# Expert layer's start: second stream's seed matmuls spread over the waits, two turned tiles in another bank, expert 0's overflow test behind expert 1's start

## Chip, core and metric

One core of a Trainium2 chip runs the kernel. The metric is the device time of one execution in microseconds; the figures shown are the median and the spread of several executions. Engine names are those of the profile: PE (TensorE matmul) and PEld (its weight load), DVE (VectorE), ACT (ScalarE), POOL (GpSimd), SP (SyncE, which here issues nearly all DMAs).

## What is computed

One layer of a hybrid model on 256 tokens of 1024 channels, float32. Four mixers and an output projection come first; then, as far as the change goes:

```python
x = x + g1 * y_x
h_x = modulate(rmsnorm(x, norm2_g), sh2, sc2)
logits = (h @ w_router + b_router)            # 256 tokens, 32 experts
top_vals, top_idx = lax.top_k(logits, 4); gates = softmax(top_vals)
# per expert e, on the tokens that chose it:
gu = xb @ w_gu[e] + b_gu[e]                   # 1024 x 2048
act = (min(up, 7) clipped + 1) * swish-like(gate)
y = act @ w_down[e] + b_down[e]               # 1024 x 1024
x = x + g2 * sum of gates * y ; return rmsnorm(x, final_norm_g)
```

All 32 experts run, so all their weights (12 MB each, 384 MB) are read once.

## The kernel before

**Weights.** The expert weights are a stream of 384 chunks of 1 MB, 12 for an expert: 8 of `w_gu` (one for each of the 8 rows of 128 of the contraction) and 4 of `w_down`. The text calls them chunk 0 to 383; chunk 12e + k belongs to expert e. They go through a ring of 18 places in SBUF (`RING`, `NSLOT`), so chunk n + 18 goes where chunk n was and can be issued only when the last reader of chunk n in the program before it is done. `load_to(n)` appends the chunks up to n to SP's queue. SP works strictly in the order of its queue: a DMA that waits for its place holds all DMAs behind it. Eight DMAs can be under way (eight semaphores in turn). Places 16 and 17 of the list, the last in the ring's order, hold the two tensors `YT` (input of the output projection, chunk 16's place) and `XT` (the residual stream, transposed, chunk 17's place) until they have been read for the last time.

**Up to the first expert** (lines 795 to 1050). `finish(b)` ends the output projection and puts the new stream into `XT`, two tiles of 128 channels at a time. `natural(i)` turns tile i back to tokens on partitions, into PSUM banks 4 to 7. `squares` sums squares on ACT, `logits` multiplies by the router; a square root on ACT and a short Newton step on DVE give the norm `rs2`. DVE then makes the logits `LG`, the eight largest (`max`), a mask of the top four (`match_replace`, `MK`, its copy `MB` in bf16), PE ranks the tokens of each expert by matmuls with triangular ones (lines 871 to 875), and DVE makes of the rank `PM` a one-hot matrix (line 911). `pick` (line 929) gathers the tokens of an expert by matmul with the one-hot from `H`, the normed stream, which ACT copies out of the banks of `natural`. `picked` copies the result to SBUF, `turn_rows` transposes it and DVE applies scale and shift: `XET`, the input of `gate_up`. `seed(c)` multiplies the stream's tiles by the identity into the four banks in which the experts' outputs are summed up later; it is the last reader of `XT`.

**The experts.** `gate_up(e)` (line 956) is 32 matmuls (64 in the profile, since float32 takes two passes), `down(e)` (line 980) half as many. An expert has room for 64 tokens. If more chose it, `block(e, 64)` runs the expert a second time on the rest; that is a branch on a count, taken at run time by PE, DVE and ACT (`tc.If`, line 1060). In each turn e of the loop stands, in this order: `down(e - 1)`, the loads of the next chunks, the test and block of expert e, the sum of expert e - 1, `gate_up(e)`, the pick of the next expert, the swish, the next turn of rows and of the activations. So before the first `gate_up` PE meets the test of expert 0.

A chunk's readers, in the order of the program, are the block of its expert (when it is taken) and `gate_up` or `down` of it. Where the branch is not taken, PE adds what the block would have added to its semaphore, once all of its work ahead of the branch is done.

Of the kernel before, what the change touches and what calls it, by code (L numbers as in the profile page):

```python
# [10 lines left out]
ALU = mybir.AluOpType  # L11
# [56 lines left out]
def tile_hybrid_moe(tc, x, ctx, vec, mats, const, pos_col, pos_row, rows, bias, w_mod, w_in, w_out,  # L68
# [4 lines left out]
    with tc.tile_pool(name="big", bufs=1) as big, tc.tile_pool(name="acc", bufs=1, space=PSUM) as acc_pool, \  # L73
# [10 lines left out]
        def R(off, n):  # L84
            return B[:, off:off + n]
# [719 lines left out]
        def natural(i):  # L805

            for c in range(2):
                pe.transpose(N[c][i // 4][:, (i % 4) * P:(i % 4 + 1) * P], XT[:, i, c * P:(c + 1) * P], ident)

        def seed(c):  # L810

            for i in range(KT):
                pe.matmul(Y[c][i // 4][:, (i % 4) * P:(i % 4 + 1) * P], XT[:, i, c * P:(c + 1) * P], ident,
                          start=(i % 4 == 0), stop=False)

        def logits(k):
# [26 lines left out]
        dve.scalar_tensor_tensor(ssq[:, 0, :], ssq[:, 0, :], EPS, ssq[:, 1, :], op0=ALU.add, op1=ALU.add)  # L843
# [4 lines left out]
        w2 = ssq[:, 0, :]  # L848
        dve.tensor_tensor(out=w2, in0=w2, in1=ssq[:, 2, :], op=ALU.add)
        rsqrt_newton(rs2, w2, tn2)  # L850
        act.activation(SM[:, 1:2], epsc, AF.Exp)
        for c in range(2):
            dve.scalar_tensor_tensor(LG[:, c, :], LR[:, c, :], rs2[:, c:c + 1], LB, op0=ALU.mult, op1=ALU.add)
            for q in range(2):
                act.activation(H[:, c, cols2[q]], N[c][q], AF.Copy, scale=rs2[:, c:c + 1])
            dve.max(out=M8[:, c, :], in_=LG[:, c, :])
        dve.tensor_scalar(nm, M8[:, :, 0], -1.0, None, op0=ALU.mult)
# [74 lines left out]
        def picked():  # L932
            act.activation(XE, mis[0], AF.Copy)  # L933

        def turn_rows(dst, ps):
# [3 lines left out]
            d4 = dst.rearrange("p j (g s) -> p j g s", g=2)  # L939
            dve.tensor_tensor(out=d4, in0=ps.rearrange("p (j g s) -> p j g s", j=4, g=2),  # L940
                              in1=jg(A2c).unsqueeze(3).to_broadcast([P, 4, 2, CAP]), op=ALU.mult)
            dve.tensor_tensor(out=d4, in0=d4, in1=jg(SH2c).unsqueeze(3).to_broadcast([P, 4, 2, CAP]), op=ALU.add)
# [307 lines left out]
```

## Time and profile before

| | |
|---|---|
| median of 3 executions | 1122.84 us (1119.83 to 1123.47) |
| profiled execution | 1123.31 us, of which span 1121.4 us |
| PE busy | 1036.5 us, 92% of the span |
| DVE, ACT, POOL busy | 305.3, 128.7, 34.9 us |
| DMA | 445.47 MB, mean 397 GB/s |

Times in the profile count from the start of the span. The parts of the span: up to some 160 us the mixers and the output projection, then some 12 us up to the first `gate_up`, then 32 experts. In one expert the branch is taken, at about 386 us. A table by windows gives for each stretch the busy time of the engines, the clock that TensorE was granted (1.00 is 2.4 GHz, 0.50 is 1.2 GHz) and the rate at which the DMA engines moved bytes.

### The profile page before, as it was taken

The page shows a single profiled execution, that of the slowest core. Times are in us where ns is not written, and L with a number is a line of the kernel's source. Part 1 is how long each engine was busy: PE and PEld are TensorE (multiplying, and loading weights), DVE is VectorE, ACT ScalarE, POOL GpSimd, SP SyncE. Part 2 cuts the span into 40 slices and gives each one's busy share as a digit, 9 for nine tenths or more (in the row PEclk, how much of TensorE's full clock was granted, in tenths as well). Part 3 has the DMA queues.
Part 4 walks back from the last instruction along what each step waited for, and adds up shares of the span by engine and source line. Part 5 has one row for each costly group of instructions (what it writes and reads, how often), then busy time and mean ns, then how long its engine had stood idle before and what let it go on. Part 6 is the DMA issues. An engine that isn't in the chain of part 4 may idle for free. (4 is left out here: it accounts for less than half of the span.)

```text
span 1121.4 us, 12287 instructions
## 1 busy us (share of the span) xinstructions
PE 1036.5 (92%) x4888; PEld 424.1 (38%) x4888; DVE 305.3 (27%) x588; ACT 128.7 (11%) x239; POOL 34.9 (3%) x77
## 2 busy tenths in 40 slices
PE   4999989999999989999999998999989898989995
PEld 2665864333333333333333333333323232323232
DVE  5488742122222212221212121212121112111122
ACT  4133430000000000000000000000000000000002
POOL 4102120000000000000000000000000000000000
PEclk8999998999999999999999999999999999999999
DMA  9987988999999998999999999999999999999994
GB/s 293 375 352 314 411 335 337 391 419 420 420 420 421 422 389 356 420 421 420 419 420 421 420 421 420 420 420 420 421 420 420 422 420 419 421 420 420 421 405 159
DMA packets 71148, 445.47 MB, mean 397 GB/s; under 512 B 7748, under 2 KB 9732, under 8 KB 20360
## 3 DMA queue, kind: packets, MB, share of 16 engines
q1 hardware_dynamic: 70408, 443.44, 96.5%
q8 instruction: 71, 1.16, 0.4%
q0 software_dynamic: 640, 0.63, 0.2%
q14 instruction: 29, 0.24, 0.1%
HBM read 442.40 MB, written 1.05 MB: 395 GB/s over the span
## 5 line engine op out<-in xcount | busy, mean ns | idle before, releaser
L956 PE MATMUL bank<-B 128*64 128x512 f32 x2112 | 473.4, 596 | 35.4 <-DMA B<-in_w_gu_dram 34.1
L956 PEld LDWEIGHTS bank<-B 128*64 128x64 f32 x2112 | 160.4, 137 | 329.1 <-issue 224.2
L980 PE MATMUL bank<-B 128*64 128x512 f32 x1024 | 228.2, 598 | 2.7 <-DMA B<-in_w_down_dram 1.8
L960 DVE TENSOR_SCALAR B<-bank 128x512 f32<-128x512 f32 x33 | 22.8, 692 | 464.3 <-issue 404.0
L980 PEld LDWEIGHTS bank<-B 128*64 128x64 f32 x1024 | 71.6, 138 | 139.7 <-issue 127.6
L961 ACT ACTIVATE B<-B 128x512 f32<-128x512 f32 x33 | 20.8, 630 | 765.6 <-DVE B L960 765.6
L1004 DVE TENSOR_TENSOR B<-bank,B 64x512 f32<-64x512 f32 x64 | 44.0, 688 | 223.1 <-PE bank L980 222.3
L1008 PE MATMUL bank<-B 128*128 128x512 f32 (+2 forms) x140 | 69.7, 606 | 3.2 <-PEq L1107 2.3
L929 PE MATMUL bank<-B 128*64 128x512 f32 x264 | 63.4, 599 | 0.9 <-DVE B L866 0.9
L945 PE MATMUL bank<-T,E 96*64 96x512 bf16 x196 | 33.6, 389 | 6.4 <-PEq L1060 4.8
L1008 PEld LDWEIGHTS bank<-B 128*128 128x128 f32 x140 | 22.7, 191 | 38.3 <-issue 25.7
L380 PE MATMUL bank<-B 128*128 128x256 f32 x160 | 36.8, 385 | 0.0
L940 DVE TENSOR_TENSOR B<-bank,B 128x512 f32<-128x512 f32 x33 | 22.8, 692 | 42.7 <-PE bank L937 42.7
L929 PEld LDWEIGHTS bank<-B 128*64 128x64 f32 x264 | 20.4, 137 | 36.6 <-issue 35.6
L380 PEld LDWEIGHTS bank<-B 128*128 128x128 f32 x160 | 30.9, 194 | 8.4 <-issue 4.5
L945 PEld LDWEIGHTS <-E 96*64 96x64 bf16 x196 | 10.6, 106 | 46.1 <-issue 45.1
L973 ACT ACTIVATE B<-bank 128x512 f32<-128x512 f32 x33 | 19.7, 597 | 55.8 <-PE bank L972 55.8
L933 ACT ACTIVATE B<-bank 128x512 f32<-128x512 f32 x33 | 19.7, 597 | 47.5 <-PE bank L929 47.5
L937 PEld LDWEIGHTS bank<-B 128*128 128x128 f32 x132 | 16.5, 143 | 22.4 <-ACT B L933 20.6
L962 DVE TENSOR_SCALAR B<-bank 128x512 f32<-128x512 f32 x33 | 22.8, 692 | 3.7 <-PE bank L956 0.6
L964 DVE SCALAR_TENSOR_TENSOR B<-B 128x512 f32<-128x512 f32 x33 | 22.8, 692 | 3.4
L535 DVE SCALAR_TENSOR_TENSOR B<-B 128x256 f32<-128x256 f32 x58 | 23.2, 481 | 0.0
(273 smaller groups left out, 534.3 us busy)
## 6 DMA issues: line engine op xcount, KB each, us to landing
B<-in_w_gu_dram SPq DMA_DIRECT2D x256, 1024.0 KB, 19.8
B<-in_w_down_dram SPq DMA_DIRECT2D x127, 1024.0 KB, 20.0
B<-in_w_mod_dram SPq DMA_DIRECT2D x16, 1024.0 KB, 6.6
B<-in_w_mod_dram SPq DMA_DIRECT2D x16, 512.0 KB, 10.0
B<-in_w_out_dram SPq DMA_DIRECT2D x4, 1024.0 KB, 8.9
B<-in_w_in_dram SPq DMA_DIRECT2D x8, 384.0 KB, 7.6
B<-in_w_in_dram SPq DMA_DIRECT2D x8, 256.0 KB, 5.4
B<-in_ctx_dram SPq DMA_DIRECT2D x1, 1024.0 KB, 6.2
```

Of the source, the lines that this page charges most:

```text
L380: pe.matmul(half(b, t), w, UT[:, k, 256:512], start=(k == 0 and t == 0), stop=(k == KT - 1 and t == 1))
L535: dve.scalar_tensor_tensor(dst, src, w, dst, op0=ALU.mult, op1=ALU.add)
L929: pe.matmul(mis[0][64 * g:64 * g + 64, :], p[:, c, :], H[:, c, 512 * g:512 * g + 512], start=(c == 0), stop=(c == 1))
L940: dve.tensor_tensor(out=d4, in0=ps.rearrange("p (j g s) -> p j g s", j=4, g=2), in1=jg(A2c).unsqueeze(3).to_broadcast([P, 4, 2, CAP]), op= ...
L945: pe.matmul(dst[64 * g:64 * g + 64, :], E3[:, e:e + 1].to_broadcast([96, CAP]), T[:, col:col + 512], start=True, stop=False)
L956: pe.matmul(dst[64 * g:64 * g + 64, :], xt[:, k % 4, (k // 4) * 64:(k // 4) * 64 + 64], w[:, b * 1024 + g * 512:b * 1024 + g * 512 + 512], ...
L960: dve.tensor_scalar(GH, G0, 7.0, 0.5, op0=ALU.min, op1=ALU.mult)
L962: dve.tensor_scalar(UP, G1, 7.0, -7.0, op0=ALU.min, op1=ALU.max)
L964: dve.scalar_tensor_tensor(UP, TH, 1.0, UP, op0=ALU.add, op1=ALU.mult)
L980: pe.matmul(dst[64 * g:64 * g + 64, :], AT[:, k % 4, (k // 4) * 64:(k // 4) * 64 + 64], dn[e, k, g], start=False, stop=(k == KT - 1))
L1004: dve.tensor_tensor(out=dst[p0:p0 + 64, 512 * g:512 * g + 512], in0=ps[64 * g:64 * g + 64, :], in1=G2B[64 * g:64 * g + 64, :], op=ALU.mult)
L1008: pe.matmul(Y[c][q][:, a:b], s[:, c * P:(c + 1) * P], o[:, 512 * q + a:512 * q + b], start=False, stop=last)
```

## The change

- `natural(6)` and `natural(7)` write to bank 2 (`N6`, free since `finish(2)`) in place of the second halves of banks 5 and 7. Their squares stand ahead of the copy of the logits on ACT.
- The mask: the top four are copied to a tile `W8` whose other entries are set at the start; `MB` comes straight from the comparison in bf16; the memset and the cast between them are gone. The load of the exponential's table on ACT stands behind the copies of `H`, of which there are now six.
- The one-hot of the first pair of experts is made in two instructions of half the size; the pick of expert 0 waits for the first.
- `turn_rows` of expert 0 works in two halves, and `gate_up(0)` takes the chunks in the order 0, 1, 4, 5, 2, 3, 6, 7.
- The seed matmuls, before eight tiles of one token half at a time, are spread: tiles 4 to 7 behind the router's second product, 0 and 1 ahead of the pick, 2 and 3 behind it, tiles 0 to 2 of the second half behind the turned rows, tiles 3 to 7 behind `gate_up(0)` and the pick of expert 1.
- Chunk 17, whose place is `XT`, is loaded by a `load_to` behind these last seeds; before the loop stands `load_to(NSLOT - 1)`.
- Expert 0's test and block stand in turn 1, behind `down(0)` and ahead of the loads of that turn.

The diff, cut to its core:

```diff
-        def seed(c):
-            for i in range(KT):
+        def seed(c, tiles_):
+            for i in tiles_:
                 pe.matmul(Y[c][i // 4][:, (i % 4) * P:(i % 4 + 1) * P], XT[:, i, c * P:(c + 1) * P], ident, ...)
...
         for k in range(4, KT):
             logits(k)
+        squares(2, N6)
         act.activation(LT, bank[0][:, 0:256], AF.Copy)
...
-        squares(2, 1, 256, 512)
-        seed(0)
+        seed(0, range(4, KT))
         rsqrt_newton(rs2, w2, tn2)
-        act.activation(SM[:, 1:2], epsc, AF.Exp)
         for c in range(2):
             dve.scalar_tensor_tensor(LG[:, c, :], LR[:, c, :], rs2[:, c:c + 1], LB, op0=ALU.mult, op1=ALU.add)
...
-        dve.memset(M8[:, :, TOPK:8], 3.0e38)
         for c in range(2):
-            dve.match_replace(out=MK[:, c, :], in_to_replace=M8[:, c, :], ...)
-        dve.tensor_tensor(out=MK, in0=MK, in1=LG, op=ALU.not_equal)
-        dve.tensor_copy(MB, MK)
+            dve.tensor_copy(W8[:, c, 0:TOPK], M8[:, c, 0:TOPK])
+            dve.match_replace(out=MK[:, c, :], in_to_replace=W8[:, c, :], ...)
+        dve.tensor_tensor(out=MB, in0=MK, in1=LG, op=ALU.not_equal)
+        dve.tensor_tensor(out=MK, in0=MK, in1=LG, op=ALU.not_equal)
+        act.activation(SM[:, 1:2], epsc, AF.Exp)
...
-        one_hot(0)
+        for i in range(2):
+            dve.tensor_tensor(out=PP[0][:, :, i, :], ...)
+        seed(0, range(2))
+        pick(PP[0][:, :, 0, :])
+        picked()
+        seed(0, range(2, 4))
         gates(0)
         gates(1)
...
-        pick(PP[0][:, :, 0, :])
-        picked()
-        turn_rows(XET, mis[1])
-        seed(1)
+        turn_rows(XET, mis[1], 2)
+        seed(1, range(3))
...
-        load_to(NSLOT)
+        load_to(NSLOT - 1)
...
-            if e < NE - 2:
-                r = nc.values_load(CNT[0:1, e:e + 1], ...)
+            tests = [(i, nc.values_load(CNT[0:1, i:i + 1], ...))
+                     for i in ([0, 1] if e == 1 else [e] if 0 < e < NE - 2 else [])]
             if e > 0:
                 down(e - 1, mis[1])
+            for i, r in tests[:-1]:
+                with tc.If(r > CAP):
+                    block(i, CAP)
+            if e > 0:
                 load_to(e * NCH + NSLOT)
-            if e < NE - 2:
+            for i, r in tests[-1:]:
                 with tc.If(r > CAP):
-                    block(e, CAP)
+                    block(i, CAP)
...
             picked()
+            if e == 0:
+                seed(1, range(3, KT))
+                load_to(NSLOT)
```

Three places show how the instructions now stand. The first is SP's queue at chunks 12 to 24 (L568 loads `w_gu`, L582 `w_down`; the branch row marks where the test of expert 0 stands in the queue, and SP does not wait at it). Before:

```order
L568 DMA B<-in_w_gu_dram 128x2048 x3
L1060 UNCONDITIONAL_BRANCH
L568 DMA B<-in_w_gu_dram 128x2048 x5
L582 DMA B<-in_w_down_dram 128x2048 x4
L568 DMA B<-in_w_gu_dram 128x2048
```

After the change:

```order
L568 DMA B<-in_w_gu_dram 128x2048 x6
L1074 UNCONDITIONAL_BRANCH
L568 DMA B<-in_w_gu_dram 128x2048 x2
L582 DMA B<-in_w_down_dram 128x2048 x4
L568 DMA B<-in_w_gu_dram 128x2048
```

The order of the chunks is the same, but the branch of expert 0, which stood between chunks 14 and 15, now stands between chunks 17 and 18: in the program, chunk 18 comes behind expert 0's block.

The second place is PE from the ranks (the bf16 row) to the first expert. L929 is the pick, L937 the turned rows, L813 the seeds (banks 2 and 3 first token half, 6 and 7 second), L1055 and L1060 the test. Before:

```order
L875 MATMUL bank_71<-MB,OB 32x32
L929 MATMUL bank_70<-B 64x512 x4
L937 MATMUL bank_71<-B 128x128 x4
L813 MATMUL bank_76<-B 128x128 x4
L813 MATMUL bank_77<-B 128x128 x4
L1055 TENSOR_LOAD CNT
L1055 ISA x2
L1060 COMPARE_AND_BRANCH
```

After the change (L935 pick, L943 turned rows, L818 seeds, L953 the bias matmuls of `gate_up(0)`):

```order
L881 MATMUL bank_71<-MB,OB 32x32
L818 MATMUL bank_72<-B 128x128 x2
L935 MATMUL bank_70<-B 64x512 x4
L818 MATMUL bank_72<-B 128x128 x2
L943 MATMUL bank_71<-B 128x128 x4
L818 MATMUL bank_76<-B 128x128 x3
L953 LDWEIGHTS E_65
L953 MATMUL bank_74<-T,E_65 64x512
```

Five of the eight seeds of the second half have left this place, and so has the test.

The third place is PE between the pick of expert 1 and the next branch. L980 is `down(0)`. Before:

```order
L929 MATMUL bank_70<-B 64x512 x4
L937 MATMUL bank_71<-B 128x128 x4
L972 MATMUL bank_70<-B 128x128 x4
L922 MATMUL bank_75<-B 128x128 x2
L1055 TENSOR_LOAD CNT
L1055 ISA x2
L945 LDWEIGHTS E_65
L945 MATMUL bank_71<-T,E_65 64x512
L945 LDWEIGHTS E_65
L945 MATMUL bank_71<-T,E_65 64x512
L980 MATMUL bank_71<-B 64x512 x16
L1060 COMPARE_AND_BRANCH
```

After the change, from the pick on:

```order
L935 MATMUL bank_70<-B 64x512 x4
L818 MATMUL bank_76<-B 128x128
L818 MATMUL bank_77<-B 128x128 x4
L943 MATMUL bank_71<-B 128x128 x4
L982 MATMUL bank_70<-B 128x128 x4
L928 MATMUL bank_75<-B 128x128 x2
L1069 TENSOR_LOAD CNT
L1069 ISA x2
L1069 TENSOR_LOAD CNT
L1069 ISA x2
```

Behind these rows stand, as before, the two bias matmuls and the 16 of `down(0)`, and then L1074, the branch of expert 0, where before the branch of expert 1 stood. The five seeds stand between the pick and the turned rows, and a second count is loaded.

## Rows read from the trace of the kernel before

**Rows 1.** Waits of PE from 660 to 1085 us: total us, times, longest.

```profile
PE bank L956 <- DMA B<-in_w_gu_dram: 34.1, 59, 1.3
```

**Rows 2.** DMA issues, page part 6: engine, count, KB each, us to landing.

```profile
B<-in_w_gu_dram SPq DMA_DIRECT2D x256, 1024.0 KB, 19.8
```

**Rows 3.** Windows: us, busy times, then TensorE clock, DMA share, GB/s.

```profile
160.00:163.00 3.00, 1.02 (x11) 0.70 (x10) 2.16 (x15) 2.99 (x6) 0.00 (x0) 1.00 0.83 347
160.00:175.00 15.00, 11.23 (x55) 6.84 (x56) 5.71 (x30) 4.22 (x9) 0.95 (x1) 0.77 0.33 120
195.00:205.00 10.00, 9.84 (x49) 3.38 (x47) 1.37 (x2) 0.00 (x0) 0.00 (x0) 0.97 0.88 313
205.00:412.00 207.00, 200.63 (x944) 76.86 (x942) 44.25 (x68) 15.98 (x29) 0.00 (x0) 1.00 1.01 421
412.00:430.00 18.00, 17.12 (x76) 5.83 (x74) 2.75 (x4) 0.00 (x0) 0.00 (x0) 1.00 0.69 269
422.00:424.00 2.00, 2.00 (x12) 0.66 (x10) 0.00 (x0) 0.00 (x0) 0.00 (x0) 1.00 0.29 33
424.00:425.00 1.00, 1.00 (x8) 0.32 (x6) 0.00 (x0) 0.00 (x0) 0.00 (x0) 1.00 0.43 156
660.00:1085.00 425.00, 387.71 (x1748) 131.18 (x1748) 81.97 (x124) 27.45 (x49) 0.00 (x0) 1.00 1.01 420
```

**Rows 4.** SP's timeline, three single issues: start us, us.

```profile
171.76 0.33 SPq L568 DMA_DIRECT2D B<-in_w_gu_dram  x1
...
174.40 0.33 SPq L568 DMA_DIRECT2D B<-in_w_gu_dram  x1
...
422.82 0.33 SPq L568 DMA_DIRECT2D B<-in_w_gu_dram  x1
```

**Rows 5.** PE's timeline: start us, us, line, count, [idle before, releaser].

```profile
156.02 0.33 PE L808 MATMUL bank<-B 128*128 128x128 f32 x1 [0.52 <-ACT B L822]
156.53 0.55 PE L808 MATMUL bank<-B 128*128 128x128 f32 x3 [0.18 <-ACT B L822]
...
158.61 2.03 PE L813 MATMUL bank<-B 128*128 128x128 f32 x16
162.57 0.18 PE L871 MATMUL bank<-MB,UB 128*128 128x32 bf16 x1 [1.92 <-DVE MB L863]
...
163.81 2.71 PE L929 MATMUL bank<-B 128*64 128x512 f32 x8 [0.86 <-DVE B L866]
167.20 1.11 PE L937 MATMUL bank<-B 128*128 128x128 f32 x4 [0.69 <-ACT B L933]
168.10 3.62 PE L813 MATMUL bank<-B 128*128 128x128 f32 x16
172.02 0.62 PE L945 MATMUL bank<-T,E 96*64 96x512 bf16 x4 [0.30 <-PEq L1060]
172.45 13.93 PE L956 MATMUL bank<-B 128*64 128x512 f32 x64
...
186.19 1.91 PE L929 MATMUL bank<-B 128*64 128x512 f32 x8
...
191.29 0.44 PE L922 MATMUL bank<-B 128*128 128x128 f32 x2 [1.37 <-DVE B L917]
192.00 0.54 PE L945 MATMUL bank<-T,E 96*64 96x512 bf16 x2 [0.28 <-issue]
192.32 8.65 PE L980 MATMUL bank<-B 128*64 128x512 f32 x32
201.13 0.62 PE L945 MATMUL bank<-T,E 96*64 96x512 bf16 x4 [0.16 <-PEq L1060]
...
379.25 7.09 PE L980 MATMUL bank<-B 128*64 128x512 f32 x32
```

**Rows 6.** DVE's and ACT's timelines in the same form.

```profile
162.32 0.20 DVE L863 CAST MB<-B 128x64 bf16<-128x64 f32 x1
...
163.23 0.42 DVE L911 TENSOR_TENSOR B<-B 128x256 f32<-128x256 f32 x1
...
168.35 0.69 DVE L940 TENSOR_TENSOR B<-bank,B 128x512 f32<-128x512 f32 x1 [2.93 <-PE bank L937]
...
157.71 0.38 ACT L842 ACTIVATE B<-bank 128x256 f32<-128x256 f32 x1 [1.24 <-PE bank L818]
157.99 0.38 ACT L822 ACTIVATE B<-bank 128x256 f32<-128x256 f32 x1
...
159.19 0.20 ACT L196 ACTIVATE B<-B 128x2 f32<-128x2 f32 x1 [0.23 <-DVE B L849]
159.41 1.28 ACT L851 ACT_TABLE_LOAD   x1
```

**Rows 7.** Windows again, for the clock.

```profile
165.00:171.00 6.00, 5.31 (x22) 3.81 (x19) 1.73 (x5) 0.60 (x1) 0.92 (x1) 0.50 0.02 4
192.00:195.00 3.00, 3.00 (x10) 1.17 (x12) 0.19 (x1) 0.19 (x1) 0.00 (x0) 0.52 1.02 429
```

More of the change, by code (lines that the diff above doesn't have):

```diff
@@ L779, in tile_hybrid_moe @@
         N = [[bank[4 + 2 * c + q] for q in range(2)] for c in range(2)]
+        N6 = [half(2, c) for c in range(2)]
         Y = [[bank[2], bank[3]], [bank[6], bank[7]]]
@@ L788, in tile_hybrid_moe @@
         jk = R(O_ACC, 512)
+        W8 = rt[:, 470:486].rearrange("p (c e) -> p c e", c=2)
+        dve.memset(W8, 3.0e38)
         GT = R(O_GATE, 64).rearrange("p (c e) -> p c e", c=2)
@@ L807, in natural @@
             for c in range(2):
-                pe.transpose(N[c][i // 4][:, (i % 4) * P:(i % 4 + 1) * P], XT[:, i, c * P:(c + 1) * P], ident)
-        def seed(c):
-            for i in range(KT):
+                dst = N6[c][:, (i - 6) * P:(i - 5) * P] if i >= 6 else N[c][i // 4][:, (i % 4) * P:(i % 4 + 1) * P]
+                pe.transpose(dst, XT[:, i, c * P:(c + 1) * P], ident)
+        def seed(c, tiles_):
+            for i in tiles_:
                 pe.matmul(Y[c][i // 4][:, (i % 4) * P:(i % 4 + 1) * P], XT[:, i, c * P:(c + 1) * P], ident,
@@ L818, in logits, with squares @@
             pe.matmul(bank[0][32 * g:32 * g + 32, 0:256], WRT[:, k, :], XT[:, k, :], start=(k < 4), stop=(k >= 4))
-        def squares(b, q, a, z):
-            for c in range(2):
-                act.activation(jk[:, a:z], N[c][q][:, a:z], AF.Square, scale=D ** -0.5, accum_out=ssq[:, b, c:c + 1])
+        def squares(b, srcs):
+            for c, src in enumerate(srcs):
+                act.activation(jk[:, 0:src.shape[1]], src, AF.Square, scale=D ** -0.5, accum_out=ssq[:, b, c:c + 1])
         finish(0)
@@ L830, in tile_hybrid_moe @@
         natural(3)
-        squares(0, 0, 0, 512)
+        squares(0, [N[c][0] for c in range(2)])
         for k in range(4):
@@ L836, in tile_hybrid_moe @@
         natural(5)
-        squares(1, 1, 0, 256)
+        squares(1, [N[c][1][:, 0:256] for c in range(2)])
         for i in (6, 7):
@@ L841, in tile_hybrid_moe @@
             logits(k)
+        squares(2, N6)
         act.activation(LT, bank[0][:, 0:256], AF.Copy)
-        dve.scalar_tensor_tensor(ssq[:, 0, :], ssq[:, 0, :], EPS, ssq[:, 1, :], op0=ALU.add, op1=ALU.add)
+        w2 = ssq[:, 0, :]
+        dve.scalar_tensor_tensor(w2, w2, EPS, ssq[:, 1, :], op0=ALU.add, op1=ALU.add)
+        dve.tensor_tensor(out=w2, in0=w2, in1=ssq[:, 2, :], op=ALU.add)
         for c in range(2):
             pe.matmul(LR[:, c, :], LT[:, c * P:(c + 1) * P], E32, start=True, stop=True)
-        squares(2, 1, 256, 512)
-        seed(0)
-        w2 = ssq[:, 0, :]
-        dve.tensor_tensor(out=w2, in0=w2, in1=ssq[:, 2, :], op=ALU.add)
+        seed(0, range(4, KT))
         rsqrt_newton(rs2, w2, tn2)
+        for c in range(2):
+            dve.scalar_tensor_tensor(LG[:, c, :], LR[:, c, :], rs2[:, c:c + 1], LB, op0=ALU.mult, op1=ALU.add)
+            for a, z, src in ((0, 512, N[c][0]), (512, 768, N[c][1][:, 0:256]), (768, 1024, N6[c])):
+                act.activation(H[:, c, a:z], src, AF.Copy, scale=rs2[:, c:c + 1])
+            dve.max(out=M8[:, c, :], in_=LG[:, c, :])
+        for c in range(2):
+            dve.tensor_copy(W8[:, c, 0:TOPK], M8[:, c, 0:TOPK])
+            dve.match_replace(out=MK[:, c, :], in_to_replace=W8[:, c, :], in_values=LG[:, c, :], imm_value=-3.0e38)
+        dve.tensor_tensor(out=MB, in0=MK, in1=LG, op=ALU.not_equal)
+        dve.tensor_tensor(out=MK, in0=MK, in1=LG, op=ALU.not_equal)
+        dve.tensor_scalar(nm, M8[:, :, 0], -1.0, None, op0=ALU.mult)
         act.activation(SM[:, 1:2], epsc, AF.Exp)
         for c in range(2):
[L853 to L857, printed above, removed]
-        dve.memset(M8[:, :, TOPK:8], 3.0e38)
-        for c in range(2):
-            dve.match_replace(out=MK[:, c, :], in_to_replace=M8[:, c, :], in_values=LG[:, c, :], imm_value=-3.0e38)
             act.activation(EX[:, c, :], LG[:, c, :], AF.Exp, bias=nm[:, c:c + 1])
-        dve.tensor_tensor(out=MK, in0=MK, in1=LG, op=ALU.not_equal)
-        dve.tensor_copy(MB, MK)
         def gates(c):
@@ L933, in picked, with turn_rows @@
             act.activation(XE, mis[0], AF.Copy)
-        def turn_rows(dst, ps):
+        def turn_rows(dst, ps, parts_=1):
             for j in range(4):
                 pe.transpose(ps[:, j * P:(j + 1) * P], XE[:, j * P:(j + 1) * P], ident)
[L939 to L942, printed above, removed]
+            d4, s4 = dst.rearrange("p j (g s) -> p j g s", g=2), ps.rearrange("p (j g s) -> p j g s", j=4, g=2)
+            n = 4 // parts_
+            for j in range(0, 4, n):
+                col = lambda ap: jg(ap)[:, j:j + n].unsqueeze(3).to_broadcast([P, n, 2, CAP])
+                dve.tensor_tensor(out=d4[:, j:j + n], in0=s4[:, j:j + n], in1=col(A2c), op=ALU.mult)
+                dve.tensor_tensor(out=d4[:, j:j + n], in0=d4[:, j:j + n], in1=col(SH2c), op=ALU.add)
         def bias_mm(dst, e, col, g):
@@ L951, in gate_up @@
                     bias_mm(dst, e, b * 1024 + g * 512, g)
-            for k in range(KT):
+            ks = (0, 1, 4, 5, 2, 3, 6, 7) if e == 0 else range(KT)
+            for k in ks:
                 w = wt[e, k]
@@ L1032, in tile_hybrid_moe @@
         engines = [ENG.PE, ENG.DVE, ENG.Activation]
-        one_hot(0)
+        for i in range(2):
+            dve.tensor_tensor(out=PP[0][:, :, i, :], in0=iota[:, 0:CAP].unsqueeze(1).to_broadcast([P, 2, CAP]),
+                              in1=PM[:, :, i:i + 1].to_broadcast([P, 2, CAP]), op=ALU.is_equal)
+        seed(0, range(2))
+        pick(PP[0][:, :, 0, :])
+        picked()
+        seed(0, range(2, 4))
         gates(0)
@@ L1053, in tile_hybrid_moe @@
             pr, par = divmod(e, 2)
-            if e < NE - 2:
-                r = nc.values_load(CNT[0:1, e:e + 1], min_val=0, max_val=L, engines=engines)
+            tests = [(i, nc.values_load(CNT[0:1, i:i + 1], min_val=0, max_val=L, engines=engines))
+                     for i in ([0, 1] if e == 1 else [e] if 0 < e < NE - 2 else [])]
             if e > 0:
                 down(e - 1, mis[1])
+            for i, r in tests[:-1]:
+                with tc.If(r > CAP):
+                    block(i, CAP)
+            if e > 0:
                 load_to(e * NCH + NSLOT)
-            if e < NE - 2:
+            for i, r in tests[-1:]:
                 with tc.If(r > CAP):
-                    block(e, CAP)
+                    block(i, CAP)
             if e > 0:
```

## The prediction, made before the changed kernel was run

> **What bounds the kernel now.** I read the table by windows first, the DMA column with it, then PE's waits, and last the single issues on SP.
>
> From 205 us on the stream moves 421 GB/s with a DMA share of 1.01, and 420 GB/s from 660 to 1085 us [rows 3]. A chunk of 1.0486 MB therefore costs 1.0486/421 = 2.49 us, an expert of 12 chunks 29.9 us. PE's busy time from 660 us is 387.71 of 425 us, so 29.9 × 0.912 = 27.3 us for an expert. PE is the faster of the two, and the groups of PE's waits say so from the other side: 34.1 us of waits on `w_gu`, 59 of them [rows 1]. The end is thus set by the stream. What counts is only the time in which the stream moves too little; PE's time before that matters where it holds the stream up.
>
> Such time is found in the windows [rows 3] as length × (1 − rate/421). From 160 to 175 us: 15 × (1 − 120/421) = 10.7 us. From 195 to 205: 10 × (1 − 313/421) = 2.6. From 412 to 430, behind the taken block, when the ring is full: 18 × (1 − 269/421) = 6.5. Together **19.8 us**; the long windows show nothing lost.
>
> The first of these is the place of the change. The engines ran dry at 160 + 3 × 347/421 = 162.5 us. Chunk 17 went out at 171.76, right behind the last seeds (168.10 + 3.62 = 171.72), and chunk 18 at 174.40 [rows 4, 5], when `gate_up(0)`, begun at 172.45, was through its first chunk. What an issue takes until the stream flows is seen at 422.82 [rows 4]: by 425 us only (2 × 33 + 1 × 156)/421 = 0.53 us worth of full rate had been moved [rows 3], so full rate began, in effect, at 424.47, that is 1.65 us after the issue. The 19.8 us from issue to landing of a `w_gu` load [rows 2] is the wait behind others in a full queue; it doesn't apply to an empty one.
>
> **The change, part by part.** *What releases chunk 18.* This decides the sum. Chunk 18 goes where chunk 0 was and waits for the last reader of chunk 0 ahead of it in the program. Before, the test and block of expert 0 stand ahead of `gate_up(0)`, so the last reader is the first step of `gate_up(0)`. After, the order of SP's queue shows the branch between chunks 17 and 18: block 0 is written behind `down(0)`, reads chunks 0 to 11 again, and is thus the last reader of chunks 18 to 29's places. It isn't taken (the one taken block lies at 386 us), but then PE adds the block's count to its semaphore only when its work ahead of the branch is done, `down(0)` included. SP works in order, so everything behind chunk 18 stands still too. Let S be the end of `down(0)`. Then the stream is dry from 162.5 to S + 1.65, but for one chunk, 17, worth 2.49 us, which goes out behind the last seeds at some 186 us. The loss is S + 1.65 − 162.5 − 2.49 = S − 163.3, and against before
>
> change in time = S − 163.3 − 19.8 = **S − 183.1**,
>
> if the other two losses of before don't come back (below). Before, S is 192.32 + 8.65 = 200.97 [rows 5]. With no gain of PE the price would be 17.9 us.
>
> *The route to the one-hot.* The two waits of `natural(6)` and `(7)` for ACT, 0.52 and 0.18 us [rows 5], go. The squares no longer stand behind the copy of the logits, so the root, at 159.19, comes some 1.2 us earlier (157.71 to 157.99 is the copy's place; the wait of 0.7 before it goes as well) [rows 6]. The cast of 0.20 us goes with its gap to the ranks at 162.57 (162.32 to 162.57, 0.25); two small copies take the memset's place. The first one-hot is half of an operation of 0.42 us; I take 0.3 of gain, since half the elements save at most 0.21 of it and a table load of 1.28 us no longer stands on ACT before the copies of `H` [rows 6]. Sum 1.2 + 0.25 + 0.3 = 1.75: the pick starts at 163.81 − 1.75 = 162.05.
>
> *From there to `gate_up(0)`*, durations from [rows 5], where the clock was 0.50 from 165 to 171 us [rows 7]. Pick 2.71; in its wait for the copies (0.69) now stand four seed matmuls, 3.62/16 = 0.23 each, 0.9 in all; turned rows 0.90 (167.20 to 168.10); six seeds, 1.36; bias 0.43 (172.02 to 172.45). DVE's two operations of 0.69 [rows 6], halved, lie beside the seeds. The last five seeds and the test with its 0.30 us are no longer here. So 162.05 + 6.3 = 168.4. PE now reaches `gate_up(0)` sooner than the clock came back before, 171 us; at half clock from 168.4 to some 170.5 it loses 1 us, so that the start is 169.4 in effect (before: 172.45).
>
> *From there to S*: 28.52 us before. Added are five seeds (10 × 0.127 = 1.3 us at full clock, the rate of the 16 in 2.03 at 158.61), partly in the wait for `picked` of 0.69 us seen at the first pick: 0.5 to 0.6 net. A second count is loaded: one takes from 191.29 + 0.44 to 192.00, 0.3 to 0.7 us; I take 0.6. The 28.52 holds a `down(0)` of 8.65 us against 7.09 for another [rows 5], 1.6 us for a clock of 0.52 from 192 to 195 [rows 7]. I leave that in, since PE's waits ahead of it (1.37, 0.28) stay. So 28.5 + 1.1 = 29.6 and S = 169.4 + 29.6 = **199.0**, change 199.0 − 183.1 = **+15.9 us**.
>
> *Bounds of S.* If the spread seeds keep the clock at 1.00, the start is 166.6 (pick 1.91 as at 186.19, seeds at 0.127, 162.05 + 4.5) and the rest 29.6 − 1.6 = 28.0: S = 194.6, +11.5. If only the head's gain arrives, 172.45 − 1.75 + 29.6 = 200.3, +17.2. I take 199.0, nearest to the rows at 0.50 and 0.52. Those rows follow PE idling 1.92 and 0.86 us [rows 5]; after the change both gaps are about as long, less the seeds. The 0.50 held on to 171 us, though PE was at work again from 163.81. The Trainium skill (TensorE: Matmul & The Clock Gate, "What's actually happening") says that the throttled state is the default and that activity releases it; by that rule seeds set into the gaps keep the clock released, and the change comes to +11.5 instead of +15.9 us.
>
> *Behind S.* The stream must not stop again. It asks for a place each 2.49 us, PE gives one each 27.3/12 = 2.3, and PE soon waits for the stream, about from expert 4, where before it did so from some 660 us. At the taken block (expert 8), chunk 107 lands at S + 1.65 + 90 × 2.49 = 424.8; a `down` of 7.09 and one step of `gate_up`, 13.93/8 = 1.74, give chunk 96's place back at 433.6. The stream wants it when chunk 113 is nearly in, 200.65 + 96 × 2.49 − 1.65 = 438.0. A margin of 4 us: the 6.5 us of before don't come back, and neither do the 2.6 of 195 to 205, which lie in the standstill. Chunks 12 to 17 lie ready for `gate_up(1)`, so PE doesn't stop at S.
>
> **The rivals.** *The stream isn't held by the block* (not slower, the other side, and the case in which the change does only what its text says). If chunk 18 waits for `gate_up(0)` alone, it follows chunk 17, at x = 168.4 to 169.4 + 13.9 + 1.9 + 1.3 = 185.5 to 186.5, at best 183.6 with the full clock. The loss is x + 1.65 − 162.5, against 19.8: +2.9 to +5.9 us, 1125.7 to 1128.7. It decides at x = 180.6, below which it is faster; within 0.3% (3.4 us, about what a measurement of this kernel can tell from no change) it is below x = 184.0. Against it speaks the order on SP.
>
> *PE's path sets the end* (faster). S falls from 201.0 to 199.0, at best 194.6, and if every later start follows, the time falls by 2.0 to 6.4 us, 1116.4 to 1120.8. Against it: PE's 34.1 us of waits on `w_gu`, and the stream at 420 GB/s to the end. The Trainium skill (Perfetto Trace Analysis, "Optimization Strategies") sets the matmul engine's utilization as the goal, which the change raises; by that rule it would win these 2 to 6 us.
>
> *The block's margin fails.* Were the ring full again at the block, up to 6.5 us more: 1138.7 + 6.5 = 1145.2. The 4 us speak against it.
>
> **How the numbers follow.** The profiled execution took 1123.31 us, 0.47 above the median, and 1.9 above its span; 1123.31 + 15.9 = 1139.2, and from the median 1122.84 + 15.9 = **1138.7**. Its own range by the bounds of S is 1134.3 to 1140.0; the executions before spread by 3.6 us, so I widen it to 1131 to 1142, which also covers what lies between. Chances: forecast 0.85, stream not held 0.07 (some 0.03 of it within 0.3%), PE's path 0.04 (0.03 faster, 0.01 within 0.3%), the margin 0.04. So faster 0.03, same 0.04, slower 0.93.
>
> **What would show it.** Right: DMA near 0 GB/s from 163 us to the end of `down(0)`, but for one chunk; chunk 17 issued near 186, chunk 18 just behind the end of `down(0)`, near 199; no dip of the rate behind the block; PE's waits on `w_gu` from expert 3 to 5 on, in sum more than 34.1 us by far. The clock row from 163 to 171 us tells which end of S holds. Wrong: chunk 18 issued before `down(0)` ends, a rate under 415 GB/s anywhere behind 205 us, or PE without waits.

## The result and the profile of the changed kernel

| | before | changed |
|---|---|---|
| median | 1122.71 us (1119.83 to 1123.47) | 1138.33 us (1136.95 to 1139.55) |
| ratio to before, 95% interval | | 1.0145, 1.0121 to 1.0169 |
| profiled execution, its span | 1123.31, 1121.4 us | 1136.95, 1135.2 us |
| PE busy | 1036.5 us | 1039.6 us |

The change costs 15.6 us; 15.9 had been forecast (1138.7 us, range 1131 to 1142). All four executions lie in the range.

The table by windows of the changed kernel (length, busy times of PE, PEld, DVE, ACT and POOL, then TensorE's clock, DMA share and GB/s) answers to [rows 3]:

```profile
160.00:163.00 3.00, 3.00 (x10) 1.26 (x11) 1.52 (x12) 1.44 (x4) 0.33 (x1) 0.50 0.42 175
163.00:175.00 12.00, 12.00 (x60) 4.92 (x58) 1.73 (x5) 0.60 (x1) 0.61 (x1) 0.91 0.00 1
175.00:186.00 11.00, 9.77 (x54) 4.36 (x50) 4.41 (x8) 1.82 (x3) 0.00 (x0) 1.00 0.09 23
186.00:190.00 4.00, 2.70 (x14) 1.16 (x16) 0.84 (x3) 0.38 (x1) 0.00 (x0) 1.00 0.48 201
190.00:198.00 8.00, 7.22 (x38) 2.50 (x36) 1.37 (x2) 0.00 (x0) 0.00 (x0) 1.00 0.19 62
198.00:199.00 1.00, 1.00 (x8) 0.44 (x6) 0.00 (x0) 0.00 (x0) 0.00 (x0) 1.00 1.03 426
160.00:205.00 45.00, 41.69 (x202) 17.01 (x203) 9.87 (x27) 4.24 (x9) 0.95 (x1) 0.94 0.29 113
412.00:430.00 18.00, 14.67 (x66) 5.22 (x63) 5.19 (x8) 1.50 (x3) 0.00 (x0) 1.00 1.01 422
430.00:660.00 230.00, 228.22 (x1063) 87.54 (x1063) 49.29 (x76) 16.33 (x29) 0.00 (x0) 1.00 1.01 419
660.00:1085.00 425.00, 386.54 (x1738) 130.47 (x1735) 84.50 (x130) 28.31 (x51) 0.00 (x0) 1.00 1.01 420
```

From 163 us nothing moves but for one hump at 186 us, one chunk (11 × 23 + 4 × 201 = 1057 KB), and then nothing until about 197. From 198 us the stream runs at full rate, behind the taken block too (422 GB/s where it was 269). PE is busy for 41.69 of the 45 us: the engine that had been made denser is not the one that holds the time.

SP's timeline (start, duration) names the two issues, chunk 17 and chunk 18 (the second row holds chunks 18 and 19):

```profile
183.88 0.33 SPq L568 DMA_DIRECT2D B<-in_w_gu_dram  x1
...
195.14 0.81 SPq L568 DMA_DIRECT2D B<-in_w_gu_dram  x2
```

PE's timeline of the changed kernel (start, duration, line, count, idle time before and its releaser), from the last product of the output projection (L803) on:

```profile
144.00 3.70 PE L803 MATMUL bank<-B 128*128 128x256 f32 x16
...
158.75 0.19 PE L877 MATMUL bank<-MB,UB 128*128 128x32 bf16 x1 [1.48 <-DVE MB L864]
...
159.56 1.22 PE L818 MATMUL bank<-B 128*128 128x128 f32 x4 [0.41 <-ACT B L859]
160.71 3.68 PE L935 MATMUL bank<-B 128*64 128x512 f32 x8
...
166.92 13.90 PE L966 MATMUL bank<-B 128*64 128x512 f32 x64
180.66 1.88 PE L935 MATMUL bank<-B 128*64 128x512 f32 x8
182.47 1.38 PE L818 MATMUL bank<-B 128*128 128x128 f32 x10
183.69 0.60 PE L943 MATMUL bank<-B 128*128 128x128 f32 x4
...
187.74 0.41 PE L953 MATMUL bank<-T,E 96*64 96x512 bf16 x2 [1.16 <-issue]
187.97 7.04 PE L990 MATMUL bank<-B 128*64 128x512 f32 x32
195.79 0.62 PE L953 MATMUL bank<-T,E 96*64 96x512 bf16 x4 [0.78 <-PEq L1079]
...
258.61 1.94 PE L966 MATMUL bank<-B 128*64 128x512 f32 x8 [0.54 <-DMA B<-in_w_gu_dram]
```

`down(0)` ends at S = 187.97 + 7.04 = 195.01, and chunk 18 goes out 0.13 us behind it. Chunk 17 goes out when the last five seeds (182.47 + 1.38 = 183.85) are through. The waits of SP's queue name the same two releasers, the seeds (L818) and PE's sequencer at the branch of expert 0 (L1074):

```profile
SPq L568 <- PE bank L818: 30.1, 1, 30.1
SPq L568 <- PEq L1074: 10.9, 1, 10.9
```

### The profile page after: what moved, and what is told of

Same layout as the page of the kernel before. It is cut to its first block, busy times and chain, and to the rows that moved or that the text cites. A ratio compares the mean times of both kernels' runs of the same rounds, so it can differ in the third digit from the quotient of the medians.

```text
span 1135.2 us, 12290 instructions
## 1 busy us (share of the span) xinstructions
PE 1039.6 (92%) x4888; PEld 416.4 (37%) x4888; DVE 305.7 (27%) x593; ACT 129.0 (11%) x241; POOL 34.6 (3%) x77
## 3 DMA queue, kind: packets, MB, share of 16 engines
q8 instruction: 71, 1.16, 0.4%
## 5 line engine op out<-in xcount | busy, mean ns | idle before, releaser
L966 PEld LDWEIGHTS bank<-B 128*64 128x64 f32 x2112 | 155.0, 136 | 353.3 <-issue 210.3
L990 PEld LDWEIGHTS bank<-B 128*64 128x64 f32 x1024 | 71.0, 137 | 138.7 <-issue 127.1
L935 PE MATMUL bank<-B 128*64 128x512 f32 x264 | 64.3, 607 | 0.0
L953 PE MATMUL bank<-T,E 96*64 96x512 bf16 x196 | 33.5, 388 | 7.6 <-PEq L1079 5.2
L1018 PEld LDWEIGHTS bank<-B 128*128 128x128 f32 x140 | 22.6, 190 | 38.5 <-issue 25.8
L949 DVE TENSOR_TENSOR B<-bank,B 128x512 f32<-128x512 f32 (+1 forms) x34 | 23.0, 675 | 43.0 <-PE bank L943 43.0
L935 PEld LDWEIGHTS bank<-B 128*64 128x64 f32 x264 | 20.1, 140 | 37.1 <-issue 37.1
L380 PEld LDWEIGHTS bank<-B 128*128 128x128 f32 x160 | 30.3, 190 | 7.5 <-issue 3.7
L953 PEld LDWEIGHTS <-E 96*64 96x64 bf16 x196 | 10.6, 106 | 47.2 <-issue 46.1
L950 DVE TENSOR_TENSOR B<-B 128x512 f32<-128x512 f32 (+1 forms) x34 | 23.0, 676 | 1.2
L535 DVE SCALAR_TENSOR_TENSOR B<-B 128x256 f32<-128x256 f32 x58 | 23.2, 474 | 0.0
```

Of the source, the lines that this page charges most:

```text
L380: pe.matmul(half(b, t), w, UT[:, k, 256:512], start=(k == 0 and t == 0), stop=(k == KT - 1 and t == 1))
L535: dve.scalar_tensor_tensor(dst, src, w, dst, op0=ALU.mult, op1=ALU.add)
L935: pe.matmul(mis[0][64 * g:64 * g + 64, :], p[:, c, :], H[:, c, 512 * g:512 * g + 512], start=(c == 0), stop=(c == 1))
L949: dve.tensor_tensor(out=d4[:, j:j + n], in0=s4[:, j:j + n], in1=col(A2c), op=ALU.mult)
L950: dve.tensor_tensor(out=d4[:, j:j + n], in0=d4[:, j:j + n], in1=col(SH2c), op=ALU.add)
L990: pe.matmul(dst[64 * g:64 * g + 64, :], AT[:, k % 4, (k // 4) * 64:(k // 4) * 64 + 64], dn[e, k, g], start=False, stop=(k == KT - 1))
```

## The accounting over all profiles

The sum of the prediction says: time = a constant + the moment the engines run dry + the time lost afterwards. The dry moment is 160 + 3 × rate/421 of the window 160 to 163; the loss is 45 × (1 − rate/421) of the window 160 to 205, plus 18 × (1 − rate/421) of 412 to 430. For the changed kernel: 160 + 3 × 175/421 = 161.2; 45 × (1 − 113/421) = 32.9; none at 412. Its profiled execution took 1136.95 us, so the rest is 942.8. From the same three windows of the other profiles, their own execution's time beside them ("again" is a second profile of the same kernel; for the kernel before, 45 × (1 − 295/421) = 13.5 stands where the prediction had 10.7 + 2.6 from two shorter windows):

| kernel | time | dry | loss, 160 to 205 | loss, 412 to 430 | rest |
|---|---|---|---|---|---|
| before | 1123.31 | 162.5 | 13.5 | 6.5 | 940.8 |
| before, again | 1122.97 | 161.6 | 12.4 | 8.3 | 940.7 |
| changed | 1136.95 | 161.2 | 32.9 | 0 | 942.8 |
| changed, again | 1140.65 | 161.6 | 35.0 | 0 | 944.1 |
| test early | 1128.90 | 160.8 | 25.3 | 1.2 | 941.6 |
| seeds early | 1141.73 | 161.5 | 36.9 | 0 | 943.3 |
| both early | 1119.67 | 160.7 | 10.9 | 6.4 | 941.7 |
| only the test late | 1138.62 | 160.7 | 35.5 | 0 | 942.4 |
| delay ahead of S | 1145.90 | 160.9 | 40.5 | 0 | 944.5 |
| delay behind S | 1137.48 | 160.5 | 33.8 | 0 | 943.2 |
| delay behind S, again | 1138.38 | 160.5 | 33.9 | 0 | 944.0 |
| before, delay in turn 1 | 1125.97 | 161.0 | 10.0 | 10.2, and 2.5 ahead of it | 942.3 |
| before, delay in turn 20 | 1121.05 | 160.9 | 11.8 | 6.6 | 941.8 |
| chunk 17 behind others | 1122.44 | 161.1 | 11.2 | 5.3 | 944.8 |

The time ranges over 26 us, the rest over 4.1. Part of that rest is small losses elsewhere: in the changed kernel the window 430 to 660 shows 419 GB/s (230 × (1 − 419/421) = 1.1 us), before 421. What differs between the kernels is thus nearly all the stream's standstill.

## The experiments

Three theories were put against each other: (1) the block behind `down(0)` holds chunk 18 and with it the stream; (2) the late seeds hold it, through chunk 17; (3) PE's path sets the end. A time is compared with the kernel before on the same chip; the chips differ by up to 3.6 us (before: 1122.7, 1119.3, 1119.1 and 1120.3 us on the four used).

**Each of the two moves undone.**

```diff
 # test early: expert 0's test and block in turn 0 again
-  for i in ([0, 1] if e == 1 else [e] if 0 < e < NE - 2 else [])]
+  for i in ([e] if e < NE - 2 else [])]
```

> The changed kernel with expert 0's test and block back in turn 0, ahead of gate_up(0); the last five seeds and chunk 17 stay late. (Expert 0 has no second block with these inputs; if it had one, this order of seeds and block would not add up.) Theory 1, the block holds the stream: chunk 18 now follows chunk 17 at about 184 us instead of 195, the stream loses 184 + 1.65 - 161.4 = 24.4 us instead of 32.9, so 8.5 us less than the changed kernel: 1130 us. Theory 2, the late seeds hold the stream, through chunk 17: no gain, 1138. Theory 3, PE's path sets the end: PE's work is the same, 1138.

Measured: 1130.18 us, 1.0097 of before (1.0069 to 1.0125). SP's timeline of this kernel, one row for chunks 17, 18 and 19, and its windows:

```profile
184.70 1.28 SPq L568 DMA_DIRECT2D B<-in_w_gu_dram  x3
```

```profile
160.00:205.00 45.00, 41.28 (x202) 17.24 (x200) 9.87 (x27) 3.84 (x9) 0.95 (x1) 0.96 0.45 184
412.00:430.00 18.00, 16.73 (x64) 5.59 (x66) 2.75 (x4) 0.34 (x1) 0.00 (x0) 0.91 0.96 394
```

Chunk 18 follows chunk 17 with nothing between, 10 us sooner than in the changed kernel, and the loss falls from 32.9 to 25.3 us. At the block 1.2 us of loss come back. The 1130 us had been reckoned from the first chip; on this chip, where before takes 1119.3, that the number itself was met is luck. By the ratios (1.0097 against the changed kernel's 1.0145 and 1.0160) the move gives back 5 to 7 of the 8.5 us expected. What is left over before is the late chunk 17.

```diff
 # seeds early: the last five seeds and chunk 17 ahead of gate_up(0)
-        seed(1, range(3))
+        seed(1, range(KT))
-        load_to(NSLOT - 1)
+        load_to(NSLOT)
...
-            if e == 0:
-                seed(1, range(3, KT))
-                load_to(NSLOT)
```

> The changed kernel with the last five seeds and the load of chunk 17 back ahead of gate_up(0); expert 0's test and block stay in turn 1. Theory 1: chunk 17 goes out near 168 us, but chunk 18 still at the end of down(0), some 195 us; its 2.49 us of transfer are only moved, so the time stays at 1137 to 1140 us. Theory 2: the stream flows again from 168 us, 1119 to 1123 us. Theory 3: PE's work is the same, 1138.

Measured: 1139.93 us, 1.0177 (1.0145 to 1.0209). SP's timeline shows chunk 17 and chunk 18 far apart, PE's the `down(0)` that lies between:

```profile
168.12 0.33 SPq L568 DMA_DIRECT2D B<-in_w_gu_dram  x1
...
199.24 0.33 SPq L568 DMA_DIRECT2D B<-in_w_gu_dram  x1
```

```profile
189.38 9.73 PE L990 MATMUL bank<-B 128*64 128x512 f32 x32
```

189.38 + 9.73 = 199.11, and chunk 18 goes out at 199.24. PE's sequencer at L1074 is again what SP waits for, 30.7 us in one wait. Chunk 17, 16 us sooner than in the changed kernel, gains nothing; `down(0)` took 9.73 us where the changed kernel's profile has 7.04, which puts S later still. Theory 2 falls as the cause of the 15.6 us; it is right about test early, where the seeds are what is left.

**Both undone.** The diff is the two above together.

> The changed kernel with both back: seeds and chunk 17 ahead of gate_up(0), expert 0's test in turn 0. What is left of the change is the shorter route to the one-hot, the spread of the other seeds and the turned rows in halves. Theories 1 and 2: the stream flows again from about 169 us, as in the kernel before but some 2 us sooner; PE reaches gate_up(0) about 2 us sooner and down(0) runs at full clock (1.6 us), and since the ring is full at the taken block this reaches the end: 1118 to 1121 us. Theory 3: the end follows PE's first experts, which are not sooner than in the changed kernel: 1138.

Measured: 1119.26 us against 1119.32, 0.9993 (0.9976 to 1.0010). The loss of the change is gone, and of the shorter route to the one-hot nothing arrives that could be measured. The 1118 to 1121 us expected were a gain of 2 to 5 on the first chip's 1122.7; against before on this chip that gain did not come, and that the number was met is luck. The windows show a loss at the start of 10.9 us (13.5 before) and, again, the one at the block:

```profile
160.00:205.00 45.00, 41.71 (x201) 17.90 (x202) 9.87 (x27) 3.55 (x9) 0.95 (x1) 0.94 0.81 319
412.00:430.00 18.00, 17.16 (x74) 6.06 (x76) 2.76 (x4) 0.00 (x0) 0.00 (x0) 1.00 0.68 272
```

and PE's timeline, in front of `gate_up(0)`, a wait at the branch for DVE's sequencer:

```profile
168.04 0.62 PE L953 MATMUL bank<-T,E 96*64 96x512 bf16 x4 [0.81 <-DVEq L1079]
```

A test there makes PE wait for DVE, which must be through with both halves of the turned rows before it comes to its own branch: DVE's last operation on them ends at 167.15 us, PE goes on at 168.04. Where the late seeds don't fill the time, in test early, the same wait is 1.92 us, and PE goes on 0.9 us behind DVE's last operation again (166.40 and 167.29). In the kernel before it was 0.30 [rows 5], since the seeds covered it. From the start of the output projection's last product to that of `gate_up(0)` it is 172.45 − 146.27 = 26.2 us before, 168.47 − 143.30 = 25.2 with both early, 167.72 − 143.58 = 24.1 with test early, 168.48 − 145.28 = 23.2 with seeds early and 166.92 − 144.00 = 22.9 in the changed kernel. Of the changed kernel's gain of 3.3 us on PE, 1.2 to 2.0 thus come from having no test there, the same move that stops the stream; where the clock fell differs between these profiles and has a part in it.

Counted from the same product, S comes 195.27 − 143.30 = 52.0 us later with both early and 200.97 − 146.27 = 54.7 before, a gain of 2.7. But `down` of the taken block took 8.78 us there instead of 7.09, so that the stream begins again behind the block after 418.83 − 143.30 = 275.5 us, before after 422.82 − 146.27 = 276.6 [rows 4]. The 1.0 us that is left is less than the interval can tell.

```profile
418.83 2.04 SPq L568 DMA_DIRECT2D B<-in_w_gu_dram  x2
```

**One part alone.** Only the test, in the kernel before:

```diff
-            if e < NE - 2:
-                r = nc.values_load(CNT[0:1, e:e + 1], ...)
+            tests = [(i, nc.values_load(CNT[0:1, i:i + 1], ...))
+                     for i in ([0, 1] if e == 1 else [e] if 0 < e < NE - 2 else [])]
             if e > 0:
                 down(e - 1, mis[1])
+            for i, r in tests[:-1]:
+                with tc.If(r > CAP):
+                    block(i, CAP)
+            if e > 0:
                 load_to(e * NCH + NSLOT)
-            if e < NE - 2:
+            for i, r in tests[-1:]:
                 with tc.If(r > CAP):
-                    block(e, CAP)
+                    block(i, CAP)
```

> The kernel before with one part of the change: expert 0's test and block in turn 1, ahead of that turn's loads. Seeds, head and chunk 17 as before. Theory 1: chunk 18 waits for the end of down(0), 201 us plus some 1 us for the second count, less 0.3 for the test: S = 201.7, change S - 183.1 = +18.6 us, 1141 us. Theory 2: chunk 17 is early, so 1122 to 1123 us. Theory 3: PE has about 1 us more to do, 1124.

Measured: 1138.92 us, 1.0183 (1.0148 to 1.0218), 19.6 us over before; +18.6 had been expected. SP's and PE's timelines:

```profile
167.44 0.33 SPq L568 DMA_DIRECT2D B<-in_w_gu_dram  x1
...
197.10 0.80 SPq L568 DMA_DIRECT2D B<-in_w_gu_dram  x2
```

```profile
188.70 8.26 PE L980 MATMUL bank<-B 128*64 128x512 f32 x32
```

188.70 + 8.26 = 196.96, chunk 18 at 197.10. SP waits for PE's sequencer at the branch of expert 0 once more, 29.3 us in one wait. This one move makes the whole loss, by medians more than the whole change does (the intervals overlap). Theory 1 stands.

**Does the time follow S, or PE's path?** The same delay, four more picks (8.75 − 1.88 = 6.9 us by the trace), on either side of S in the changed kernel, in turn 0 and in turn 1:

```diff
-            pick(PP[(e + 1) // 2 % 2][:, :, (e + 1) % 2, :])
+            for _ in range(5 if e == 0 else 1):        # or: if e == 1
+                pick(PP[(e + 1) // 2 % 2][:, :, (e + 1) % 2, :])
```

> The changed kernel itself once more, as the reference on the same chip for the two delays that run with it: 15 to 20 us over the kernel before.

> The changed kernel with the pick of expert 1 done five times instead of once, between gate_up(0) and down(0): 4 x 1.88 = 7.5 us more of PE ahead of S, the end of down(0). Theory 1, the stream waits for S: the whole 7.5 us come on top of the changed kernel. Theory 3, PE's path sets the end: also +7.5. Theory 2, the late seeds: chunk 17 is later by 7.5 us too, +7.5.

> The changed kernel with the same four extra picks, 7.5 us of PE, in turn 1 instead, between gate_up(1) and down(1), behind S. Theory 1: the stream flows by then and PE has 11.7 us of waits on w_gu up to 430 us to give away, so nothing of it is seen at the end: within 2 us of the changed kernel. Theory 3, PE's path sets the end: +7.5 us, as with the delay ahead of S.

Measured beside the changed kernel's 1136.53 us (1.0160): ahead of S 1147.14 (1.0258, 1.0239 to 1.0277), behind S 1138.97 (1.0188, 1.0168 to 1.0208). The windows from 160 to 205 us of the two, the delay ahead of S first:

```profile
160.00:205.00 45.00, 41.63 (x198) 16.01 (x199) 9.87 (x27) 3.85 (x9) 0.95 (x1) 0.93 0.13 42
```

```profile
160.00:205.00 45.00, 41.60 (x196) 16.26 (x198) 9.88 (x27) 3.44 (x9) 0.95 (x1) 0.94 0.27 105
```

Ahead of S the loss grows to 40.5 us, behind it it stays at 33.8. By medians the first came out at 10.6 us, where 7.5 had been expected, and the second at 2.4, where less than 2 had. The second was run again beside other kernels:

> The changed kernel with four extra picks in turn 1 again, for a narrower interval. Theory 1, hidden: the ratio to the kernel before is that of the changed kernel, 1.015 to 1.016. Theory 3, PE's path: 1.021 to 1.022.

Measured: 1138.63 us, 1.0162 (1.0143 to 1.0181), the changed kernel's own ratio (1.0145 and 1.0160). The delay behind S is hidden; the 2.4 us did not come again. With the delay ahead of S, S comes 202.25 − 143.60 = 58.7 us behind the start of the output projection's last product, in the changed kernel's profile on that chip 197.39 − 145.50 = 51.9: 6.8 us later, as the four picks make it. Why the medians differ by some 4 us more is open; the changed kernel's four executions there spread over 4.6 us.

**Does PE's path count at all, though the stream is the bound?** Both early still shows the loss at the block. There the ring is full, so the stream begins again when PE gives a place back, and PE's path up to the block should count whole in the kernel before; a gain of 1.0 us is only too small to be seen. The same delay, in turn 1 and in turn 20 of the kernel before:

> The kernel before with the pick of the next expert done five times in turn 1, 7 us more of PE. Theory 1 with the ring: in this kernel the stream stands still at the taken block (6.5 us) because the ring is full, so what PE loses ahead of the block comes on top whole: +6 to +7 us over the kernel before, although the stream is the bound at the end. If the stream alone counted and PE's path never, +0.

> The kernel before with the same four extra picks in turn 20, behind the taken block, where PE waits for w_gu: hidden, within 2 us of the kernel before. If PE's path set the end everywhere, +7 us.

Measured: 1129.08 us in turn 1, 1.0072 (1.0049 to 1.0096), +8.8 us by medians, where 6 to 7 had been expected (the interval is 5.5 to 10.8); 1121.00 us in turn 20, 1.0000 (0.9985 to 1.0015). In turn 1 the windows are

```profile
205.00:412.00 207.00, 200.62 (x944) 76.89 (x942) 44.25 (x68) 15.97 (x29) 0.00 (x0) 1.00 1.00 416
412.00:430.00 18.00, 17.12 (x76) 5.82 (x74) 2.76 (x4) 0.00 (x0) 0.00 (x0) 1.00 0.46 183
```

The stream now loses 2.5 us ahead of the block (416 GB/s) and 10.2 at it (183 GB/s), where it lost 6.5. In this profile the clock fell at another place and S came 2.9 us sooner than before, counted from the output projection's last product (195.45 − 143.61 = 51.8 against 54.7), and the stream begins again behind the block 4.0 us later (424.16 − 143.61 = 280.6 against 276.6): the 6.9 us of the picks less the 2.9. So in the kernel before, PE's path up to the taken block does set the end; the same delay behind it, in turn 20, doesn't move it. In the changed kernel the stream comes to the block too late for the ring to be full, and there S alone counts.

**A version without either hold.** Test in turn 0, five seeds ahead of it, three behind `gate_up(0)`, and chunk 17 issued behind six others (the last part of the diff):

```diff
-                seed(1, range(3, KT))
-                load_to(NSLOT)
+                seed(1, range(5, KT))
+                for i in (18, 19, 22, 23, 20, 21, 17, 24, 25):
+                    load_chunk(i, *stream[i])
+                nxt[0] = 26
```

> The changed kernel with expert 0's test in turn 0, five seeds of the second half ahead of it and three behind gate_up(0), and chunk 17 issued behind chunks 18, 19, 22, 23, 20 and 21 (in the order in which gate_up(0) gives their places back), so that neither the block nor the late seeds hold the stream. Theory 1: chunk 18 goes out near 169 us, the loss from 160 to 205 us is 9 to 11 us, and the ring is full again at the taken block, so that PE's path up to there sets the rest: 1116 to 1120 us, within 0.3% of the kernel before. Theory 2, late seeds cost by themselves: 1125 or more.

Measured: 1119.11 us against 1120.33, 0.9991 (0.9979 to 1.0003). It takes back all that the change lost, and is not to be told from the kernel before. None of the versions run is faster than that.

## Why the prediction was right, point by point

- **The release of chunk 18.** Right, and it carries the result: 0.13 us behind the end of `down(0)` in the changed kernel, and again in two experiments (0.13 and 0.14 us). Chunk 17 went out at 183.88, which is 186.2 on the scale of before (next point), forecast "some 186".
- **S.** Forecast 199.0 on the time scale of the kernel before, bounds 194.6 and 200.3. Measured 195.01; but in that execution the output projection's last product began 146.27 − 144.00 = 2.3 us sooner than in the profile of before, a product that the change doesn't touch. On the scale of before this is 197.3. The row on before, and one that the fifth point needs:

```profile
146.27 3.70 PE L799 MATMUL bank<-B 128*128 128x256 f32 x16
...
188.78 0.66 PE L937 MATMUL bank<-B 128*128 128x128 f32 x4 [0.69 <-ACT B L933]
```

- **The route to the one-hot.** The ranks came 16.30 us behind that product before (162.57 − 146.27) and 14.75 after (158.75 − 144.00): 1.55 us, where 1.2 + 0.25 = 1.45 had been summed. The pick was expected 1.75 us sooner and came 0.83 sooner (160.71 − 144.00 = 16.71 against 17.54). The one-hot was ready, both halves, at 159.94; the sum had no term for the seeds of two tiles in front of the pick: they write bank 2, from which the copies of `H` of tiles 6 and 7 must first be read (0.41 us of waiting for ACT), and take 1.22 us at half clock.
- **The clock.** The forecast was a fall as before, and a fall came, about as long (from 158 to 165 us, before from 164 to 171) but some 6 us sooner on the profile's scale. So `gate_up(0)`, which was to lose 1 us, ran its 13.90 us at full clock. With the pick's miss this cancels, by luck: `gate_up(0)` at 166.92 + 2.3 = 169.2, forecast "169.4 in effect". The second fall, 1.6 us in `down(0)`, which had been left in the sum, was absent in the profile (7.04 us) and present in the changed kernel's other profile (8.46) and in the other kernels with a late test (8.26 and 9.73 us): that is most of the 1.7 us between 199.0 and 197.3. The first fall began, by a mean of 0.67 in this window, at some 158.3 us, in PE's wait of 1.48 us ahead of the ranks (an estimate from the row):

```profile
158.00:159.00 1.00, 0.25 (x5) 0.21 (x4) 0.90 (x7) 1.00 (x3) 0.00 (x0) 0.67 1.01 418
```

  By the Trainium skill (TensorE: Matmul & The Clock Gate, "What's actually happening") activity releases the throttle; the lower bound that was worked out by that rule did not come. The seeds that the change sets into the next gap ran only at 159.56, when the clock had already fallen, so whether they could have kept it up this trace doesn't show.
- **Five seeds and the second count.** From the start of the pick to that of the turned rows, 183.69 − 180.66 = 3.03 us against 188.78 − 186.19 = 2.59 before: 0.44, forecast 0.5 to 0.6. The wait before `down(0)` is 1.16 instead of 0.28 [rows 5]: 0.88, forecast 0.6.
- **The sum.** By the windows dry moment and loss grew by (161.2 + 32.9) − (162.5 + 13.5 + 6.5) = 11.6 us, with 1.1 us between 430 and 660 by 12.7, against 13.6 between the two profiled executions. The medians differ by 15.6. The forecast's +15.9 is nearer to the medians than its own terms were to the profiled pair, because that pair differs by 2.3 us ahead of the change (12.7 + 2.3 = 15.0); so the hit is as good as the mechanism and the scatter of some 2 us allow, not better.
- **Behind S.** No further stop: 422 GB/s from 412 to 430 us. PE's first wait on `w_gu` came at 258.61, in `gate_up(3)`, as forecast. That these waits would be "more than 34.1 us by far" was wrong in size. The groups of PE's waits, over the whole span and from 660 us on:

```profile
PE bank L966 <- DMA B<-in_w_gu_dram: 46.7, 83, 1.0
```

```profile
PE bank L966 <- DMA B<-in_w_gu_dram: 35.0, 61, 1.0
```

  PE falls behind at the taken block and is busy 228.22 of 230 us from 430 to 660, as before; then it waits as before. Only the 11.7 us ahead of the block are new.
- **The rivals.** That the stream isn't held was tried as test early, though with the test back ahead of `gate_up(0)`. The rival had priced +2.9 to +5.9 us with an issue at 185.5 to 186.5; the issue came at 184.70, which is 187.4 on the scale of before (146.27 − 143.58 = 2.7) and holds PE's wait of 1.92 us at the test, which the rival had no term for. The time came out at +10.9 by medians. Both early takes the time of before on that chip; against it, dry moment and loss grew by (160.8 + 25.3 + 1.2) − (160.7 + 10.9 + 6.4) = 9.3 us, and the two profiled executions differ by 9.2. That PE's path sets the end is false in the changed kernel behind S and, which the prediction hadn't weighed, true in the kernel before up to the block.

## What to carry to other kernels

Where a ring of buffers feeds an engine, the last reader in program order gives a place back, a reader in a branch that isn't taken too: a block moved behind other work moves the release of every buffer it names, and with an in-order queue of every load behind them. Look for the moved instruction in the queue that loads, not only on the engine that computes. And a stream that is the bound at the end can still be set by the compute engine wherever the ring runs full; ask at which point the two change places before an engine's gain is counted or dismissed.

## What was not expected of the hardware

A few more matmuls in the program brought new waits of PE at branches far behind them. In the kernel before with the delay in turn 20, PE's timeline shows, eight experts later,

```profile
988.56 1.06 PE L945 MATMUL bank<-T,E 96*64 96x512 bf16 x4 [2.81 <-PEq L1060]
```

and by the groups of PE's waits

```profile
PE bank L945 <- PEq L1060: 14.4, 29, 2.8
```

where the kernel before has 4.8 us, none longer than 0.3. The delays in the changed kernel show the same (12.9 and 13.4 us, 5.2 without a delay). They cost nothing here (1.0000), since PE waits for the stream there anyhow; what causes them wasn't tried. And the fall of the clock moves from execution to execution: `down(0)` took 7.04 us in one profile of the changed kernel and 8.46 in the other, and with both early the 1.7 us fell into the `down` of the taken block (8.78 us, 7.09 before) instead.
